# Chunked attention on one core: q and k transposed and split for pairs of heads, rows placed by DMA from the SyncE queue

## The chip, the cores and the metric

The kernel runs on one core of a Trainium2 chip. The metric is the device time of one execution in microseconds (us); the median of three runs of the kernel before is 1270.3 us (1268.56 to 1270.39). Engines are named as in the profile: PE is the matmul engine (PEld its weight loads), DVE is VectorE, ACT is ScalarE, POOL is GpSimd, SP is SyncE, which here only issues DMAs.

## The reference, cut to what matters

One layer of a transformer trunk on 1024 positions: a combined input projection, two groups of eight attention heads, an output projection, then a convolutional gated feed-forward layer. The two attention groups:

```python
# "mla": 8 heads, head dim 96, causal by 64-position chunks over all keys
s = einsum('bqhd,bkhd->bhqk', qb, k) * scale;  p = softmax(where(mask, s, NEG_INF));  o = p @ v
# "ca": 8 heads, head dim 64: each 64-position chunk sees itself and the 8 chunks before it
q, k = rmsnorm(q, g_ca_q), rmsnorm(k, g_ca_k)
s = einsum('bcqhd,bckhd->bhcqk', qc, kb) * scale
s = where(valid, s + rel_bias[:, clip(dist)], NEG_INF)
o = softmax(s) @ vb
...
x += concat(rmsnorm(o_a, g_out_mla), rmsnorm(o_b, g_out_ca)) @ w_out
x += conv_glu_ffn(rmsnorm(x))
```

## The kernel before, in words

Everything is float32. A product of two float32 tensors is made of three matmuls: each operand is split into a high part (rounded to the matmul's format) and a low part (the rest), and hi·hi, lo·hi and hi·lo are added in PSUM (`mm3`, lines 136 to 139). So every operand costs a rounding copy on ACT and a subtraction on DVE or POOL.

The program's order is written out by hand. The stages, with their time in the profile: latent projections and the mla up-projection (to 79 us), the projection to q, k and v of the chunked heads in 32 steps (79 to 230 us), attention (230 to 523 us), output projection (to 619 us), and the feed-forward layer, up (to 1051 us) and down (to the end).

**Attention** goes over 16 heads, `heads`, in turn ca and mla (n = 0 is ca head 0, n = 1 mla head 0, n = 2 ca head 1, ...). Each head has 12 score pieces; the program has one *slot* for each, 192 in all. In a slot PE makes the score piece (L908 to L922), ACT takes the exponential twice, a third engine forms the low part of the probabilities `plo` by a subtraction (L950: POOL from a copy in SBUF, or DVE from PSUM for the pieces listed in `PLO_V`), and PE adds the product of probabilities and v three slots later (L958 to L960, `LAG` is 3).

**Preparing a head** (`prep(n)`) is spread over the 24 slots ahead of its first score; slot m of head n's preparation is slot 12(n - 2) + m. For a ca head: 16 PE transposes of 128x64 blocks of q and k, in groups of four (L671); q's high part on ACT (L674) and low part on DVE (L678), k's likewise (L682, L688); 32 rows zeroed on POOL (`zero`, L694); q's high part copied to partitions 64 to 127 and k's high part to partitions 0 to 63 of a stacked tensor by two DMAs that POOL issues (`dup_q`, `dup_k`, L691 and L697). Then eleven passes `mx` multiply q with k (L737) and DVE takes row maxima from them (L745 for ca, L750 for mla). The maxima are transposed (L756), negated (L759) and put into a row of the operand set by a DMA that POOL issues (L760). Three operand sets `QH, QL, K1, K2` rotate over the heads; their mask rows are written once per set by ACT (`set_rows`, L612). The first two heads are prepared during the last steps of the chunked projection; their slots are given by `first_slot`, from -8 to 60.

**Ending a head** (`finish`): the sums of the exponentials are fetched by DMA (L1011), inverted on DVE (L1014), written to DRAM (L1016) and read back spread over 64 partitions (L1017); ten slots later DVE multiplies (L1023). Every second head of a kind, ACT squares the pair's outputs and DVE adds the squares up (`o_sq`, L978 and L979).

Each engine runs its instructions in order, and so does each DMA-issuing queue: a DMA on SP or POOL that waits for data holds back what stands behind it there.

## Time and profile before

| | |
|---|---|
| median of 3 runs | 1270.3 us (1268.56 to 1270.39) |
| profiled execution, its own time | 1271.62 us |
| its span from first to last instruction | 1269.9 us |
| busy PE / DVE / POOL / ACT | 1221.0 / 940.8 / 704.6 / 648.8 us |
| granted PE clock, mean over the span | 0.995 |

The span is what the trace covers; 1.7 us of the execution's time lie around it. A busy engine is one that executes an instruction; PE's matmuls are pipelined, so a busy PE can still differ in pace, and the granted clock (1 is 2.4 GHz, 0.5 is 1.2 GHz) has to be read beside it.

### The profile page before, as it was taken

What the parts mean: (1) busy time and instruction counts of PE and PEld (TensorE: products, weight loads), DVE (VectorE), ACT (ScalarE), POOL (GpSimd) and SP (SyncE); (2) the same over time, 40 slices, a digit from 0 to 9 for tenths busy, and PEclk for the clock granted to TensorE, in tenths of its full rate; (3) what the DMA queues carried; (4) which work ended last, traced back from release to release, by engine and by line L of the source; (5) the groups of instructions that cost most, each with busy time, mean ns of one, the idle gap of its engine ahead of it and who ended that gap; (6) DMA issues with size and microseconds to landing.
All of it is one profiled execution on the core that took longest, in us unless ns stands there. A gap on an engine that the chain in (4) does not pass through costs nothing.

```text
span 1269.9 us, 17774 instructions
## 1 busy us (share of the span) xinstructions
PE 1221.0 (96%) x5888; PEld 1004.7 (79%) x5888; DVE 940.8 (74%) x1623; ACT 648.8 (51%) x1338; POOL 704.6 (55%) x710
## 2 busy tenths in 40 slices
PE   9999998899998998999889999999999999999998
PEld 9888876787786876788668888888888888878887
DVE  6678565688888895466898766767776677888983
ACT  7562254678877887405555434334334344434442
POOL 4689750466564668204488767667677640425630
PEclk9999998999999999999999999999999999999999
DMA  9111213111111221265413332333322256933153
GB/s 353 36 35 50 59 56 78 26 44 43 27 37 37 43 64 52 100 232 174 141 59 121 120 99 84 108 108 105 119 81 86 91 181 243 363 92 116 59 197 127
DMA packets 102637, 134.78 MB, mean 106 GB/s; under 512 B 12152, under 2 KB 60816, under 8 KB 102544
## 3 DMA queue, kind: packets, MB, share of 16 engines
q1 hardware_dynamic: 100752, 129.37, 31.3%
q0 software_dynamic: 1792, 4.26, 1.7%
q8 instruction: 47, 0.77, 0.3%
q14 instruction: 46, 0.38, 0.1%
HBM read 97.47 MB, written 31.81 MB: 102 GB/s over the span
## 4 chain that ended last, share of the span: by engine, by line
PE 50%; DVE 8%; issue 2%; ACT 1%; POOL 1%; DVEq 0%; POOLq 0%; ACTq 0%
PE pb L139 11%; PE pb L138 11%; PE pb L137 11%; PE ps L137 6%; PE ps L139 5%; PE ps L138 5%; DVE ps L1438 1%; DVE as L1422 1%; DVE hq L1242 1%; POOL plo L950 1%; DVE wop L1359 1%; DVE h L1206 0%; DVE as L1421 0%; DVE as L1423 0%; DVE as L1424 0%
## 5 line engine op out<-in xcount | busy, mean ns | idle before, releaser
L950 POOL TENSOR_TENSOR plo<-misc,phi 128x512 fp32r<-128x512 f32 (+3 forms) x116 | 119.1, 1029 | 58.0 <-ACT phi L935 42.7
L1383 ACT ACTIVATE u<-ps,cols 128x1024 f32<-128x1024 f32 x44 | 53.2, 1208 | 178.0 <-DVE ps L1438 178.0
L137 PE MATMUL ps<-hq,wop 128*128 128x512 f32 x344 | 135.0, 393 | 2.6 <-ACT wop L1354 1.5
L139 PE MATMUL ps<-hq,wop 128*128 128x512 f32 x344 | 134.2, 390 | 1.8 <-DVE wop L1359 1.8
L138 PE MATMUL ps<-hq,wop 128*128 128x512 f32 x344 | 134.0, 390 | 0.2 <-DVE hq L1242 0.2
L138 PE MATMUL pb<-wring,aring 128*128 128x512 f32 x308 | 120.7, 392 | 2.1 <-DVE wring L1613 2.1
L137 PE MATMUL pb<-wring,aring 128*128 128x512 f32 x308 | 120.6, 391 | 0.3 <-DVE x2b L1438 0.3
L139 PE MATMUL pb<-wring,aring 128*128 128x512 f32 x308 | 120.6, 391 | 0.0
L1359 POOL TENSOR_TENSOR wop<-S,wop 128x512 fp32r<-128x512 f32 x42 | 63.3, 1507 | 96.4 <-ACT wop L1354 96.4
L137 PE MATMUL pb<-hq,wop 128*128 128x512 f32 x264 | 103.0, 390 | 2.3 <-ACT wop L1354 2.2
L139 PE MATMUL pb<-hq,wop 128*128 128x512 f32 x264 | 103.1, 390 | 0.2 <-DVE wop L1359 0.2
L138 PE MATMUL pb<-hq,wop 128*128 128x512 f32 x264 | 102.7, 389 | 0.0
L1610 DVE TENSOR_TENSOR aring<-ast,aring 128x512 fp32r<-128x512 f32 x77 | 71.1, 924 | 37.6 <-ACT aring L1609 37.6
L1609 ACT ACTIVATE aring<-ast 128x512 fp32r<-128x512 f32 x77 | 48.5, 630 | 93.7 <-PE pb L138 74.0
L932 ACT ACTIVATE misc<-pb 128x512 f32<-128x512 f32 (+3 forms) x116 | 56.3, 485 | 47.9 <-PE pb L918 20.0
L137 PEld LDWEIGHTS ps<-hq,wop 128*128 128x128 f32 x344 | 64.5, 188 | 20.0 <-DVE ps L1438 4.9
L138 PE MATMUL pb<-wl,hTh 128*128 128x512 f32 x192 | 75.8, 395 | 2.0 <-DVE wl L553 1.9
L139 PEld LDWEIGHTS ps<-hq,wop 128*128 128x128 f32 x344 | 64.6, 188 | 16.0 <-DVE wop L1359 2.5
L137 PE MATMUL pb<-wh,hTh 128*128 128x512 f32 x192 | 76.2, 397 | 0.0
L139 PE MATMUL pb<-wh,hTl 128*128 128x512 f32 x192 | 75.6, 394 | 0.0
L138 PEld LDWEIGHTS ps<-hq,wop 128*128 128x128 f32 x344 | 64.6, 188 | 13.7 <-DVE hq L1242 0.6
L204 POOL TENSOR_TENSOR stat<-stat,mhalf 128x1 f32<-128x1 f32 (+2 forms) x50 | 72.7, 1454 | 4.2
(331 smaller groups left out, 3629.8 us busy)
## 6 DMA issues: line engine op xcount, KB each, us to landing
wstage<-in_w_up_dram SPq DMA_DIRECT2D x43, 512.0 KB, 4.2
ast<-act_scratch SPq DMA_DIRECT2D x77, 256.0 KB, 4.5
act_scratch<-as SPq DMA_DIRECT2D x44, 256.0 KB, 2.3
wd<-in_w_down_dram SPq DMA_DIRECT2D x44, 256.0 KB, 5.5
act_scratch<-u SPq DMA_DIRECT2D x33, 256.0 KB, 2.1
x<-in_x_dram SPq DMA_DIRECT2D x16, 512.0 KB, 7.2
ws<-in_w_in_dram SPq DMA_DIRECT2D x32, 256.0 KB, 2.6
x_scratch<-x SPq DMA_DIRECT2D x14, 512.0 KB, 3.0
```

The source lines that it names most:

```text
L137: T.matmul(o, lh, rh, start=start, stop=False)
L138: T.matmul(o, lh, rl, start=False, stop=False)
L139: T.matmul(o, ll, rh, start=False, stop=stop)
L204: G.tensor_tensor(dst, dst, mhalf[:, :n], op=ALU.pow)
L932: A.activation(p32[:, w], o[:, w], AF.Exp, scale=sc_)
L950: e.tensor_tensor(plo[:, w], p32[:, w], f(phi[:, w]), op=ALU.subtract)
L1242: lo_eng.tensor_tensor(lo, s3[:, ks], f(hi), op=ALU.subtract)
L1359: (V if n in W_LO_V or (j, n) in W0_LO_V else G).tensor_tensor(lo, s, f(hi), op=ALU.subtract)
L1383: A.activation(u, U, AF.Identity, scale=convw(2, c), bias=convb(c))
L1422: V.tensor_tensor(s[1], s[0], A11, op=ALU.subtract)
L1609: A.activation(ah, s, AF.Copy)
L1610: V.tensor_tensor(al, s, f(ah), op=ALU.subtract)
```

## The change

Of the eight ca heads, h = 2 to 7 are prepared in pairs. The even head of a pair transposes 128x128 blocks, which hold both heads, and splits both heads' q and k at once into four staging tensors `qh, ql, kh, kl` with q and k of the even head on partitions 0 to 63 and of the odd head on 64 to 127. Each of the two heads then fetches its 64 partitions from the staging tensors by six DMAs. The odd head makes no transposes and no splits. Heads h = 0 and 1 are prepared as before. Beside that:

- DMAs that POOL issued in the attention (copies of q and k, the row of maxima) are issued by SP; the 32 zero rows come by DMA from a DRAM scratch instead of a POOL memset.
- Mask rows: POOL writes those of set 0, early; the other two sets get them from set 0 by DMA. ACT has none.
- The first head's `mx` passes use only the 64 rows of the high parts, and so read neither copy.
- The maxima passes of paired heads begin at slot 10 (even) or 7 (odd) of their preparation, not 9.
- For mla heads one more `plo` piece of 512 columns (piece 6) goes to POOL instead of DVE.
- `o_sq`: the addition comes three slots after the square (but for the last pair). `finish`: the read-back of the inverted sums is issued two slots later than the write.
- The loads of the projection's weights for steps 23 to 31 are issued one step earlier.

```diff
-PLO_V = (1, 3, 6, 8, 10)
+PLO_V = (1, 3, 6, 8, 10), (1, 3, 8, 10)
+WC_AHEAD = 20
+MX_EVEN = 10
+MX_ODD = 7
...
-    def set_rows(i):
-        st = sets[i]
+    def zero_rows():
+        st = sets[0]
+        G.memset(f(st.K2[64:96]), 0.0)
+        G.memset(f(st.QL[64:96]), 0.0)
+        nc.sync.dma_start(dzero, f(st.QL[64:96]))
+    def set_rows():
+        st = sets[0]
         for dst, c in ((st.K2, 0), (st.QL, 16)):
-            A.activation(dst[96:113].rearrange("p (t i) -> p t i", t=16),
-                         mk[96:113, c:c + 16, None].to_broadcast([17, 16, 64]), AF.Copy)
+            G.tensor_copy(dst[96:113].rearrange("p (t i) -> p t i", t=16),
+                          mk[96:113, c:c + 16, None].to_broadcast([17, 16, 64]))
+    def copy_rows(i):
+        r = 64 if heads[i][0] == "ca" else 96
+        nc.sync.dma_start(f(sets[i].K2[r:113]), f(sets[0].K2[r:113]))
+        nc.sync.dma_start(f(sets[i].QL[97:113]), f(sets[0].QL[97:113]))
...
+        def pair_tr(which, i):
+            p = hold[which, i] = bank()
+            for t in range(4):
+                T.transpose(p[:, t * 128:(t + 1) * 128], ca[which, h // 2][:, (4 * i + t) * 128:(4 * i + t + 1) * 128],
+                            ident)
+        def pair_hi(which, i):
...
+            A.activation(stg["kh" if which else "qh"][:, i * 512:i * 512 + 512], hold[which, i], AF.Copy,
+                         scale=1.0 if which else gsc[:, 1:2])
+        def pair_lo(which, i):
...
+        def send(x_):
+            o = f(stg[x_][64 * (h % 2):64 * (h % 2) + 64])
+            for d_ in {"qh": (st.QH[0:64], st.QH[64:128]), "ql": (st.QL[0:64],), "kh": (st.K2[0:64], st.K1[0:64]),
+                       "kl": (st.K1[64:128],)}[x_]:
+                nc.sync.dma_start(f(d_), o)
         def dup_q():
-            G.dma_start(st.QH[64:128], st.QH[0:64])
+            nc.sync.dma_start(f(st.QH[64:128]), f(st.QH[0:64]))
         def zero():
-            G.memset(f(st.QL[64:96]), 0.0)
+            nc.sync.dma_start(f(st.QL[64:96]), dzero)
...
-                q_, k2 = (st.QH, st.K1) if is_ca else (st.QH[0:d], st.K2[0:d])
+                q_, k2 = (st.QH, st.K1) if is_ca and n else (st.QH[0:d], st.K2[0:d])
...
-            G.dma_start(st.QL[96:97].rearrange("p (t s) -> p t s", t=8), mrow)
+            nc.sync.dma_start(f(st.QL[96:97]).rearrange("p (t s) -> p t s", t=8), f(mrow))
...
+        paired = is_ca and h > 1
+        if paired and h % 2:
+            mx_at = MX_ODD
+            r = [(0, "post", lambda: send("qh")), (1, "post", lambda: send("kh")), (2, "post", lambda: send("kl")),
+                 (3, "post", lambda: send("ql"))]
...
+            if paired:
+                mx_at = MX_EVEN
+                r += [(4, "post", lambda: send("qh")), (5, "post", lambda: send("kh")),
+                      (6, "post", lambda: send("kl")), (7, "post", lambda: send("ql"))]
...
-            micro[16, 9, 0, 0] = [lambda: set_rows(0)]
-            micro[26, 9, 0, 0] = [lambda: set_rows(1)]
+            micro[9, 9, 0, 0] = [set_rows]
+            micro[20, 9, 0, 0] = [lambda: copy_rows(1)]
...
-        return s % 12 in PLO_V if n < 14 else s in END_PLO_V
+        return s % 12 in PLO_V[n % 2] if n < 14 else s in END_PLO_V
...
+        if j < 3:
+            at(s0 + 3, add)
...
+        at(s + (5 if n < 14 else 3), spread)
```

The rows below are the program's own order, without times. The first two pieces are PE's around the first maxima pass of head 0, in step 26 of the chunked projection (`wh`, `wl` are its weights, `hTh`, `hTl` the input's parts, `set` an operand set); what an instruction waits for stands in brackets, DMASW being DMAs issued by POOL. Before:

```order
L138 MATMUL pb_2018<-wl_2046,hTh_96 128x512
L139 MATMUL pb_2018<-wh_2045,hTl_97 128x512
L737 MATMUL pb_2080<-set_2021 128x256 [waits DMASW1_49,DMASW0_49,DVE_49]
L737 MATMUL pb_2080<-set_2021 128x256
L737 MATMUL pb_2083<-set_2021 128x384
L137 MATMUL pb_2019<-wh_2045,hTh_96 128x512
```

and after, where the pass is on L783:

```order
L140 MATMUL pb_2020<-wl_2049,hTh_96 128x512
L141 MATMUL pb_2020<-wh_2048,hTl_97 128x512
L783 MATMUL pb_2085<-set_2023 128x256 x2
L783 MATMUL pb_2088<-set_2023 128x384
L139 MATMUL pb_2021<-wh_2048,hTh_96 128x512
```

The pass stands at the same place among the projection's matmuls; its wait for two DMAs is gone.

The next two pieces are POOL's while head 2 is scored and head 4 (the first even head of a pair) is prepared; `plo` is the low part of the probabilities, `vset` v's low part. Before:

```order
L950 TENSOR_TENSOR plo_2790<-misc_2284,phi_2766 128x512
L694 MEMSET set_2023 32x1024
L950 TENSOR_TENSOR plo_2838<-misc_2284,phi_2810 128x256
...
L709 TENSOR_TENSOR vset_2361<-nqk_604,vset_2361 128x128
L691 DMA set_2023<-set_2023 64x1024
L950 TENSOR_TENSOR plo_2895<-misc_2284,phi_2867 128x512
L697 DMA set_2023<-set_2023 64x1024
L950 TENSOR_TENSOR plo_2913<-misc_2284,phi_2892 128x512
L760 DMA set_2021<-mrow 1x8x128
L950 TENSOR_TENSOR plo_2946<-misc_2284,phi_2927 128x256
```

and after (L950 has become L1018, L709 L755):

```order
L1018 TENSOR_TENSOR plo_2790<-misc_2285,phi_2766 128x512
L1018 TENSOR_TENSOR plo_2840<-misc_2285,phi_2810 128x256
...
L755 TENSOR_TENSOR vset_2362<-nqk_604,vset_2362 128x128
L1018 TENSOR_TENSOR plo_2900<-misc_2285,phi_2869 128x512
L1018 TENSOR_TENSOR plo_2918<-misc_2285,phi_2897 128x512
L1018 TENSOR_TENSOR plo_2954<-misc_2285,phi_2933 128x256
```

The memset and the three DMAs that stood between the subtractions have left POOL.

The last two pieces are SP's at the same place: the bias table of head 4, the sums of head 1 (`den`) and their way through DRAM, and after the change the rows of head 4 out of the staging tensors. Before:

```order
L712 DMA misc_2284<-bias_scratch 128x256
L1011 DMA den<-misc_2284 128x1x8
L1016 DMA den_scratch<-den 128x8
L1017 DMA misc_2284<-den_scratch 64x1024
L712 DMA misc_2284<-bias_scratch 128x256
```

and after (L758 is the bias table, L740 the zero rows, L734 `send`, L806 the row of maxima of head 3, L1087 to L1094 the sums):

```order
L758 DMA misc_2285<-bias_scratch 128x256
L740 DMA set_2024<-zero_scratch 32x1024
L1087 DMA den<-misc_2285 128x1x8
L734 DMA set_2024<-stage_2822 64x1024 x2
L734 DMA set_2024<-stage_2881 64x1024 x2
L1091 DMA den_scratch<-den 128x8
L734 DMA set_2024<-stage_2882 64x1024
L758 DMA misc_2285<-bias_scratch 128x256
L806 DMA set_2023<-mrow 1x8x128
L734 DMA set_2024<-stage_2823 64x1024
L1094 DMA misc_2285<-den_scratch 64x1024
```

Five DMAs have become thirteen, and the read-back of the sums now stands behind the sends and the row of maxima.

## Rows read from the trace of the kernel before

**Rows 1.** Windows: length, busy PE, PEld, DVE, ACT, POOL; clock, DMA share, GB/s.

```profile
199.30:230.10 30.80, 24.12 (x105) 18.94 (x105) 17.18 (x51) 11.22 (x19) 0.65 (x2) 0.89 0.18 44
230.10:483.70 253.60, 237.79 (x1448) 192.69 (x1447) 213.25 (x575) 202.00 (x496) 155.97 (x203) 1.00 0.19 43
266.40:300.80 34.40, 33.33 (x211) 27.79 (x210) 28.82 (x81) 26.97 (x67) 21.10 (x30) 1.00 0.18 40
371.30:409.80 38.50, 34.66 (x211) 27.43 (x209) 33.72 (x87) 29.83 (x73) 20.72 (x29) 1.00 0.17 35
444.50:483.70 39.20, 35.07 (x210) 27.34 (x209) 34.61 (x85) 31.90 (x77) 28.92 (x37) 1.00 0.26 72
```

**Rows 2.** Timeline: PE's two waits for copies; start, us, what, idle before.

```profile
202.97 0.55 PE L737 MATMUL pb<-set 128*128 128x256 f32 x1 [3.61 <-DMA set<-set]
...
245.87 0.65 PE L737 MATMUL pb<-set 128*128 128x256 f32 x3 [1.05 <-DMA set<-set]
```

**Rows 3.** Busy time of 2 us stretches after the first wait; clock third from last.

```profile
202.00:204.00 2.00, 1.03 (x4) 1.07 (x5) 0.23 (x2) 0.61 (x1) 0.00 (x0) 0.50 0.46 136
...
208.00:210.00 2.00, 2.00 (x11) 1.64 (x11) 0.63 (x2) 0.75 (x2) 0.00 (x0) 0.80 0.29 106
```

**Rows 4.** Timeline, 212 to 216 us: ACT, DVE, PE.

```profile
212.07 2.00 ACT L612 ACTIVATE set<-mk 17x1024 fp32r<-17x1024 f32 x2
...
214.59 0.42 DVE L720 TENSOR_TENSOR bl<-tb,bh 128x256 fp32r<-128x256 f32 x1 [2.61 <-issue]
...
215.61 0.44 PE L737 MATMUL pb<-set 128*128 128x384 f32 x1 [1.63 <-DVE mcol L745]
```

**Rows 5.** Timeline of PE: one group of four transposes.

```profile
447.07 0.60 PE L671 MATMUL pb<-identr,ca 128*64 128x128 f32 x4
447.42 0.36 PE L908 MATMUL pb<-set 128*128 128x256 f32 x1
447.63 0.28 PE L916 MATMUL pb<-bh,identr 128*128 128x256 f32 x1
447.74 0.29 PE L916 MATMUL pb<-bl,identr 128*128 128x256 f32 x1
```

**Rows 6.** Timeline of PE: four transposes of 128x128 blocks, elsewhere.

```profile
610.30 0.63 PE L1256 MATMUL pb<-identr,h 128*128 128x128 f32 x4 [0.37 <-DVE h L1206]
```

**Rows 7.** Timeline of POOL and PE around two of PE's waits.

```profile
277.19 0.56 POOL L697 DMA_DIRECT2D set<-set  x1 [1.05 <-ACT phi L927]
...
279.10 0.45 PE L960 MATMUL pb<-plo,vset 128*66 128x512 f32 x1 [1.07 <-POOL plo L950]
...
422.75 0.45 PE L960 MATMUL pb<-plo,vset 128*66 128x512 f32 x1 [1.07 <-POOL plo L950]
```

**Rows 8.** Groups by form, 230 to 490 us: count, busy us, mean ns, idle before.

```profile
L950 POOL TENSOR_TENSOR plo<-misc,phi 128x512 fp32r<-128x512 f32 x50 | 66.6, 1333 | 43.0 <-ACT phi L935 30.3 <-PE pb L922 10.3 <-PE pb L960 2.2
...
L678 DVE SCALAR_TENSOR_TENSOR set<-pb,gsc,set 64x512 fp32r<-64x512 f32 x14 | 10.3, 733 | 0.0
...
L950 DVE TENSOR_TENSOR plo<-pb,phi 128x512 fp32r<-128x512 f32 x14 | 9.5, 680 | 0.9 <-ACT pb L928 0.9
...
L979 DVE TENSOR_TENSOR sqs<-sqs,sq 128x512 f32<-128x512 f32 x6 | 7.3, 1223 | 3.6 <-ACT sq L978 3.6
```

**Rows 9.** DMA issues: count, KB each, median us from issue to landing.

```profile
set<-set POOLq DMA_DIRECT2D x16, 256.0 KB, 3.0
...
misc<-den_scratch SPq DMA_DIRECT2D x16, 256.0 KB, 3.5
```

**Rows 10.** Timeline: last low part of head 4's k; its tenth slot.

```profile
276.92 0.68 DVE L688 TENSOR_TENSOR set<-pb,set 64x512 fp32r<-64x512 f32 x1 [0.74 <-ACT set L682]
...
280.80 0.28 PE L908 MATMUL pb<-set 128*128 128x256 f32 x1
```

**Rows 11.** Timeline: head 0's read-back issued, its first multiplication.

```profile
259.56 0.48 SPq L1017 DMA_DIRECT2D misc<-den_scratch  x1
...
267.21 0.69 DVE L1023 TENSOR_TENSOR op<-misc 64x512 f32<-64x512 f32 x1
```

More of the change, by code (lines that the diff above doesn't have):

```diff
@@ L650, in pieces @@
         return r
+    stg = {}
     def prep(n):
@@ L767, in prep @@
         if is_ca:
-            r += [(1, "post", zero), (4, "post", dup_q), (5, "post", dup_k), (-1, "post", lambda: bias_load(0)), (6, "post", bias_nat),
+            if n:
+                r += [(1, "post", zero)]
+            r += [(-1, "post", lambda: bias_load(0)), (6, "post", bias_nat),
                   (6, "post", lambda: bias_load(1)), (14, "post", bias_tr)]
         for j in range(11):
-            m = min((MX_CA if is_ca else 6) + max(j - 1, 0), 17)
+            m = min(mx_at + max(j - 1, 0), 17)
@@ L818, in trunk @@
     for i, (c, k, ts) in enumerate(steps):
-        if i + 2 < len(steps):
+        if i == WC_AHEAD:
             load_wc(i + 2)
+        if i + 2 + (i >= WC_AHEAD) < len(steps):
+            load_wc(i + 2 + (i >= WC_AHEAD))
         if i < 4:
@@ L891, in trunk @@
     new_set(2)
-    set_rows(2)
+    copy_rows(2)
     opair, O, wo, sqs = {}, {}, {}, {}
@@ L973, in o_sq, with add @@
             A.activation(sqs[kind][:, w], o, AF.Square)
-        else:
-            if c == 0:
-                opair["sq"] = blk(F32, "sq")
-            sq = opair["sq"][:, w]
-            A.activation(sq, o, AF.Square)
-            (G if (kind, j) in OSQ_G else V).tensor_tensor(sqs[kind][:, w], sqs[kind][:, w], sq, op=ALU.add)
+            return
+        if c == 0:
+            opair["sq"] = blk(F32, "sq")
+        sq = opair["sq"][:, w]
+        A.activation(sq, o, AF.Square)
+        def add():
+            (G if (kind, j) in OSQ_G else V).tensor_tensor(sqs[kind][:, w], sqs[kind][:, w], sq, op=ALU.add)
+        if j < 3:
+            at(s0 + 3, add)
+        else:
+            add()
     def o_part(kind, j, c):
@@ L1014, in rec, with spread @@
             V.reciprocal(d8, d8)
-            row = dden[n]
-            nc.sync.dma_start(row.rearrange("(p c) -> p c", c=8), d8)
-            nc.sync.dma_start(R[64:128], dap(row, 0, [[0, 64], [1, 1024]]))
+            nc.sync.dma_start(dden[n].rearrange("(p c) -> p c", c=8), d8)
+        def spread():
+            nc.sync.dma_start(R[64:128], dap(dden[n], 0, [[0, 64], [1, 1024]]))
         def mul(c):
```

54 lines of the change are left out of this document (36 added, 18 removed).

## The prediction

> **What bounds the kernel now.** I read the windows first, because the change touches one part of the program, the end of the chunked projection and the attention. In the attention's main stretch PE is busy 237.8 of 253.6 us, DVE 213.3, ACT 202.0 and POOL 156.0 [rows 1]. So PE sets the pace there, with 15.8 us of idle time, and DVE at 84% is the next engine. Time comes off the end in two ways: PE work that goes away, and PE waits that go away. Two pairs of heads look different from the rest: heads 2 and 3 leave PE idle 34.40 - 33.33 = 1.1 us, heads 8 and 9 3.8 us and heads 12 and 13 4.1 us [rows 1]. The stretch before, 199.3 to 230.1, in which the last projection steps and the preparation of heads 0 and 1 lie, is worse: 24.1 of 30.8 us busy at a mean clock of 0.89, while no other engine is busy more than 17.2 us [rows 1]. It is a chain of waits, not a full engine.
>
> Then the timeline, for what ends these waits. The first maxima pass of head 0 waits 3.61 us for a copy that POOL issued, and a pass of head 2 waits 1.05 us for another [rows 2]. After the first of them the clock stands at 0.50 from 202 us and at 0.80 in 208 to 210 [rows 3]: some 6.8 us at 1.2 GHz, in which PE does 3.4 us less than at 2.4. At 215.61 PE waits 1.63 us for DVE, which had stood still 2.61 us until ACT wrote a bias tile, and ACT had spent 2.0 us just before on the mask rows of L612 [rows 4]. In the attention POOL, in order, stands 1.05 us before the DMA of L697, the subtraction behind it comes late, and PE waits 1.07 us at 279.10 [rows 7]. There are four such waits of 0.9 to 1.07 us, in heads 2, 4, 6 and 10, the last at 422.75.
>
> **Term 1, the first stretch: 7.5 us.** The first pass no longer waits for the copies, so the 3.61 us go, and with them the clock's 3.4. ACT no longer writes mask rows (POOL does; it is busy 0.65 us in this stretch, so that costs nothing), so the wait at 215.61 should go: 1.6. That is 8.6. I take 7.5, as something else may become late: the weights of the next step came in at about the same time as the copy. They are now ordered a step earlier, which is why I don't take less. Bounds: 3, if those weights stop PE instead; 10.1, if PE works without a wait (30.8 minus the 24.1 less 3.4).
>
> **Term 2, transposes: 5.4 us.** Three pairs of heads make 16 transposes each where they made 32: 48 fewer, 12 groups of four. From the first transpose of a group at 447.07 to the matmul after next at 447.63 are 0.56 us, of which the matmul between takes 0.11 (447.63 to 447.74) [rows 5]: 0.45 a group, 12 of them 5.4. As busy time the same group counts 0.60, so 7.2 is the upper bound; the lower, if PE's time here is not what holds the end, is a rival below. The transposes that stay are twice as wide in their weights. Four of 128x128 take 0.63 us elsewhere, against 0.60 for four of 128x64 [rows 5, 6], so I add nothing.
>
> The Trainium skill speaks against that: "TensorE: Matmul & The Clock Gate", in the section on LDWEIGHTS, gives the load a time of columns / 1.2 in ns, so 107 instead of 53 ns for the wide blocks. Were the loads what paces them, the 48 transposes left would cost 2.6 us more and term 2 would be 2.8. The trace does not agree: 0.63 against 0.60 us for four.
>
> **Term 3, DMAs off POOL: 5 us.** The four waits of rows 7 and head 2's wait of 1.05 us [rows 2] come from POOL's order, and no DMA and no memset is left between its subtractions. In exchange POOL makes seven subtractions of 512 columns more, 1.33 us each [rows 8], one in each mla head; it has 97 us idle in the stretch [rows 1] and the new piece lies between pieces that were already its own, so I price them at nothing. If the cover is too thin, each could cost PE what a late one costs now, 1.07. Bounds 0 to 5.2.
>
> **Term 4, less work on DVE and later sums: 3.5 us.** Twelve splits of 0.73 us on 64 partitions go (24 become 12 of 128 partitions; the time goes by columns), 8.8 us, and seven subtractions of 0.68, 4.8 us [rows 8]. That is 13 of DVE's 213 us, worth nothing in itself, as DVE is not the bound. But heads 8, 9, 12 and 13 are those in which the sums of squares run: six additions of 1.22 us, before which DVE stands 3.6 us for ACT's squares [rows 8]. These four heads have 8.0 - 2 x 1.1 = 5.8 us more idle PE time than heads 2 and 3. The additions now come three slots (4.3 us at 34.4 / 24 a slot) after the squares, so DVE doesn't stand; they still cost their 1.22 us each. I take 3.5 of a possible 0 to 5.8.
>
> **Term 5, new waits: -2 us.** The low part of k is the last thing that an even head sends. In head 4 it was ready at 277.60, and slot 10, after which the first pass now comes, began at 280.80 [rows 10]. The pass itself starts some 0.5 us later, at 281.3, but 1.1 us earlier once the wait at 279.10 is gone: 280.2. A DMA takes 3.0 us to land [rows 9] and the queue some 0.5: 281.1. So 0.9 us late in each of three even heads, less what DVE gains by term 4: I take 2 in all, bounds 0 to 6. An odd head sends everything in slots 0 to 3 and begins in slot 7, four slots or 5.7 us later, which covers it. The mask rows of sets 1 and 2 are sent well ahead of their heads' scores; the zero rows also lie in slot 1 of 24. Nothing for these.
>
> Sum: 7.5 + 5.4 + 5 + 3.5 - 2 = 19.4. From the profiled execution's own 1271.6 that leaves 1252.2. The median of the runs is 1.3 us below the profiled one; I leave that inside the range and say **1252 us**. What follows the attention is PE work that only starts earlier.
>
> **The rivals.**
> - *The attention is held by DVE and ACT, not by PE.* For it: 84% and 80% [rows 1], and each slot's chain passes through both. Against it: in heads 2 and 3 PE idles 1.1 us of 34.4. Then terms 2 and 4 give nothing: 7.5 + 5 - 2 = 10.5, **1261 us**.
> - *The first stretch only changes what it waits for,* so that the change there doesn't do what it says: the weights of the next step land at the time at which the copy did. Term 1 is then 1 and the time **1259 us**.
> - *Everything in the two stretches goes that can go:* 10.1 + 7.2 + 5.2 + 5.8 = 28.3, **1243 us**.
> - *SP's queue becomes the late one.* The read-back of a head's sums was issued at 259.56, lands 3.5 us later, and is used at 267.21: 4.1 us of cover [rows 9, 11]. Two slots later (2.9 us) leave 1.2, and it now stands behind the sends and the row of maxima. If these hold it 2 us, DVE stands 0.8 us in each of 14 heads; if all of it reaches PE, 11 us are lost: **1263 us**.
> - *Slower.* In the slots 4 to 7 of an even head six copies of 256 KB go out together. If the last needs not 3.0 but 6.0 us to land, the pass in slot 10 is 3.9 us late, the clock falls as after the first wait in rows 2 and 3 (3.4 us), and three times 7.3 take 22 of the 21.4 us that the other terms give: no change. From there it decides; at 7 us it is 25, and **1275 us**. Against it: the DMA share in the attention is 0.19 [rows 1].
>
> **How the numbers follow.** Forecast 0.60; DVE and ACT hold 0.13; first stretch 0.07; everything goes 0.10; SP's queue 0.05; slower or level 0.05. The range runs from the best case to a little beyond the queue's: **1243 to 1264**, which leaves out the last rival and part of the queue's and of the best case's spread. A measurement here can tell 0.2%, 2.5 us, from no change. All cases but the last are faster by more than that; of it and the tails of the others I give 0.05 to no change and 0.03 to slower: 0.92, 0.05, 0.03.
>
> **What the profile after would show.** Term 1: no wait of PE over 1 us around 200 us, no half clock there, the first score 7 to 9 us earlier. Term 2: 80 transposes of q and k of ca heads instead of 128, and PE's busy time in the attention 5 us lower. Term 3: no wait of PE for POOL in heads 2, 4, 6 and 10. Term 4: heads 8, 9, 12 and 13 with 2 us of idle PE time or less a pair. Term 5: PE waits for the sent rows at the first pass of heads 4, 8 and 12, of about 1 us. Wrong I would be if a wait of several us stands at one of those three passes, if PE waits for weights near 203 us, or if DVE waits for the read-back in each head.

## The result and the profile after

Eight timed executions of the changed kernel have a median of 1261.2 us (1257.1 to 1266.5), eight of the kernel before on the same chip 1272.3 us (1268.6 to 1274.0). The ratio is 0.9914, interval 0.9899 to 0.993: about 11 us faster. 1252 us were forecast, with a range of 1243 to 1264. The profiled execution of the changed kernel took 1257.13 us (span 1255.4), its fastest.

Windows of the changed kernel (length, busy PE, PEld, DVE, ACT, POOL, clock, DMA share, GB/s): the 30.8 us ahead of the first score, the attention from there to head 14, heads 2 and 3, 6 and 7, 8 and 9, 12 and 13.

```profile
193.20:223.96 30.76, 29.47 (x128) 20.76 (x127) 22.17 (x59) 10.92 (x22) 2.69 (x4) 1.00 0.23 65
223.96:468.48 244.52, 231.11 (x1401) 190.14 (x1399) 197.04 (x551) 193.12 (x482) 141.88 (x173) 0.99 0.32 75
257.01:294.45 37.44, 34.84 (x210) 29.07 (x209) 28.72 (x79) 26.75 (x67) 18.93 (x25) 0.95 0.31 68
327.15:363.55 36.40, 33.31 (x211) 27.98 (x209) 28.38 (x79) 26.77 (x67) 18.96 (x25) 1.00 0.31 71
363.55:395.80 32.25, 31.93 (x195) 26.17 (x193) 27.45 (x79) 27.72 (x69) 19.40 (x25) 1.00 0.34 77
431.69:468.48 36.79, 33.41 (x195) 25.84 (x193) 28.79 (x77) 29.97 (x73) 26.53 (x29) 1.00 0.43 111
```

Against [rows 1] the first score comes at 223.96 in place of 230.10 with the clock at 1.00 in place of 0.89; the attention is 9.1 us shorter; heads 8 and 9 take 32.25 us where they took 38.50, with 0.3 us of idle PE where there were 3.8. But heads 2 and 3 take 37.44 where they took 34.40. There, and in heads 6 and 7 and 10 and 11, which also prepare the even head of a pair, time was lost.

The timeline of PE in the changed kernel, at the first maxima pass of heads 4, 8 and 12 (start, us, instruction, idle time before it and what ended it):

```profile
273.41 0.65 PE L783 MATMUL pb<-set 128*128 128x256 f32 x3 [2.60 <-DMA set<-stage]
...
344.04 0.65 PE L783 MATMUL pb<-set 128*128 128x256 f32 x3 [3.09 <-DMA set<-stage]
...
412.15 0.68 PE L783 MATMUL pb<-set 128*128 128x256 f32 x3 [2.50 <-DMA set<-stage]
```

`set<-stage` is a transfer of `send`: PE waits 8.2 us in all for rows of an even paired head. What is late shows in the same stretch in SP's queue (the x4 are q's high part twice and k's high part twice, the x1 at 269.48 is k's low part, L806 the row of maxima of head 3), on DVE, and in the DMA share (second to last column):

```profile
264.22 4.50 SPq L734 DMA_DIRECT2D set<-stage  x4
268.82 0.56 SPq L1091 DMA_DIRECT2D den_scratch<-den  x1
269.48 1.27 SPq L734 DMA_DIRECT2D set<-stage  x1
270.84 0.54 SPq L758 DMA_DIRECT2D misc<-bias_scratch  x1
271.47 0.70 SPq L806 DMA_DIRECT2D set<-mrow  x1
```

```profile
267.62 0.69 DVE L724 TENSOR_TENSOR stage<-pb,stage 128x512 fp32r<-128x512 f32 x1 [0.81 <-ACT stage L717]
...
269.25 0.27 DVE L805 TENSOR_SCALAR mrow<-pb 8x128 fp32r<-8x128 f32 x1
```

```profile
266.00:268.00 2.00, 2.00 (x16) 1.00 0.95 195
...
270.00:272.00 2.00, 0.80 (x7) 1.00 1.00 199
272.00:274.00 2.00, 0.59 (x4) 1.00 0.93 196
274.00:276.00 2.00, 2.00 (x10) 0.53 0.77 199
276.00:278.00 2.00, 2.00 (x8) 0.61 0.05 10
```

k's low part is ready at 268.31 (267.62 + 0.69), is issued 1.2 us later and has landed at 273.4, 5.1 us after it was ready. All DMA engines are busy in that time, at 195 to 199 GB/s: at that rate a transfer of 256 KB takes 1.3 us, and k's low part is the third in a row of them. After the wait the clock stands at 0.53 and 0.61.

### The profile page after: what moved, and what is told of

The parts are those of the page before. It is cut to its first block, busy times and chain, and to the rows that moved or that the text cites. A ratio compares the mean times of both kernels' runs of the same rounds, so it can differ in the third digit from the quotient of the medians.

```text
span 1255.4 us, 17692 instructions
## 1 busy us (share of the span) xinstructions
PE 1215.1 (97%) x5840; PEld 1001.0 (80%) x5840; DVE 927.3 (74%) x1603; ACT 636.1 (51%) x1320; POOL 691.2 (55%) x680
## 3 DMA queue, kind: packets, MB, share of 16 engines
q1 hardware_dynamic: 104730, 141.37, 35.9%
## 4 chain that ended last, share of the span: by engine, by line
PE 50%; DVE 7%; POOL 2%; issue 2%; ACT 1%; DMA 0%; SPq 0%; POOLq 0%; DVEq 0%; ACTq 0%
PE pb L140 11%; PE pb L139 11%; PE pb L141 11%; PE ps L139 6%; PE ps L141 5%; PE ps L140 5%; DVE as L1500 1%; DVE ps L1516 1%; DVE as L1499 0%; DMA ast<-act_scratch 0%; POOL hq L1320 0%; DVE wring L1691 0%; DVE as L1501 0%; DVE as L1502 0%; DVE h L1284 0%
## 5 line engine op out<-in xcount | busy, mean ns | idle before, releaser
L1018 POOL TENSOR_TENSOR plo<-misc,phi 128x512 fp32r<-128x512 f32 (+3 forms) x123 | 126.7, 1033 | 77.7 <-ACT phi L1003 52.2
L141 PE MATMUL ps<-hq,wop 128*128 128x512 f32 x344 | 134.2, 390 | 1.2 <-DVE wop L1437 1.2
L140 PE MATMUL ps<-hq,wop 128*128 128x512 f32 x344 | 134.0, 390 | 0.1
L140 PE MATMUL pb<-wring,aring 128*128 128x512 f32 x308 | 120.9, 393 | 2.3 <-DVE wring L1691 2.3
L141 PE MATMUL pb<-wring,aring 128*128 128x512 f32 x308 | 120.3, 391 | 0.0
L141 PE MATMUL pb<-hq,wop 128*128 128x512 f32 x264 | 103.6, 392 | 0.1
L140 PE MATMUL pb<-hq,wop 128*128 128x512 f32 x264 | 103.3, 391 | 0.0
L1000 ACT ACTIVATE misc<-pb 128x512 f32<-128x512 f32 (+3 forms) x123 | 60.6, 493 | 52.7 <-PE pb L986 24.0
L140 PE MATMUL pb<-wl,hTh 128*128 128x512 f32 x192 | 75.1, 391 | 2.0 <-DVE wl L555 2.0
L141 PEld LDWEIGHTS ps<-hq,wop 128*128 128x128 f32 x344 | 64.6, 188 | 15.2 <-DVE wop L1437 1.8
L140 PEld LDWEIGHTS ps<-hq,wop 128*128 128x128 f32 x344 | 64.6, 188 | 13.8 <-DVE hq L1320 0.6
L141 PE MATMUL pb<-wh,hTl 128*128 128x512 f32 x192 | 74.9, 390 | 0.0
```

The source lines that it names most:

```text
L140: T.matmul(o, lh, rl, start=False, stop=False)
L141: T.matmul(o, ll, rh, start=False, stop=stop)
L1000: A.activation(p32[:, w], o[:, w], AF.Exp, scale=sc_)
L1018: e.tensor_tensor(plo[:, w], p32[:, w], f(phi[:, w]), op=ALU.subtract)
```

## The experiments

Theory A: the part of the gain that is missing is this lateness, because transfers of 256 KB follow one another at 1.3 us each; and the clock that falls behind the waits in some executions makes the spread. Rivals: the wait only moves on, or something else than the transfers comes last.

All ratios are to the kernel before on the same chip. Eleven kernels that differ from the changed one and one more set of executions of it were run.

**e1_even12.** The passes of even heads begin two slots later.

```diff
-MX_EVEN = 10
+MX_EVEN = 12
```

> Edit: the changed kernel with the maxima passes of even chunked heads two units later (slot 12 in place of 10); nothing else. Theory A (the part of the gain that is missing is PE waiting for the low part of k, which is sent too late: 2.60 + 3.09 + 2.50 = 8.2 us at the first passes of heads 4, 8 and 12 in the profile of the changed kernel, and the clock that falls behind them in some executions): those three waits go or shrink below 0.5 us each, the time is 1249 to 1253 us, a ratio to before of 0.982 to 0.985, and the executions lie closer together than 1257 to 1266. Rival B (the wait only moves on: with two units less, VectorE reaches the maxima too late and PE waits for the row of maxima at the end of the same heads, or at the next head's first scores): the waits come back there, 2 to 3 us in each of the three heads, and the time stays at 1257 to 1266 us. Rival C (the spread and the missing part come from elsewhere): the waits go but the time falls by under 3 us.

1266.3 us (1263.6 to 1269.7), ratio 0.9959 (0.9945 to 0.9973): slower than the changed kernel, so theory A as I had it missed, and B is right on what happens. The waits at the passes are gone, but PE waits 2.0, 2.9 and 2.1 us at the first piece of the next head, for its row of maxima. In this kernel's timeline of PE, and of SP ahead of the first of them:

```profile
277.17 0.50 PE L990 MATMUL pb<-set 105*128 105x512 f32 x1 [2.02 <-DMA set<-mrow]
```

```profile
272.36 1.25 SPq L734 DMA_DIRECT2D set<-stage  x1
273.70 0.54 SPq L758 DMA_DIRECT2D misc<-bias_scratch  x1
274.33 0.70 SPq L806 DMA_DIRECT2D set<-mrow  x1
```

That row was ready at 272.40 and was issued at 274.33, behind k's low part. So in the changed kernel two things are late for the same reason, one behind the other, and the first wait hides the second. Behind two of the three waits the clock falls to 0.50 to 0.65. That alone does not make this kernel slower than the changed one, whose clock falls too: heads 2 and 3 take 37.69 us here with the clock at 1.00 throughout, against 37.44 there at 0.95, and PE has further waits of 0.72 and 0.31 us for DVE's maxima at 281.76 and 284.37. No run takes these apart from the rest.

**e2_order.** One transfer less ahead of k's low part.

```diff
-"ql": (st.QL[0:64],), "kh": (st.K2[0:64], st.K1[0:64]),
+"ql": ((st.QL[0:64], "ql"), (st.K2[0:64], "kh")), "kh": ((st.K1[0:64], "kh"),)
```

> Edit: the changed kernel with SP's queue in another order only: at even chunked heads the copy of the high part of k into the second tile goes out last, with the low part of q, so that one issue less stands ahead of the low part of k. Theory A (the low part of k is late, and part of that is SP's queue: in the profile of the changed kernel it was ready at 268.31 and issued at 269.48 while two copies and a scratch write were issued ahead of it): it is issued 0.5 to 1 us earlier, the three waits of 2.5 to 3.1 us become 1.5 to 2.5 us, and the time falls by 2 to 4 us against the changed kernel, to 1256 to 1260 us in the median. Rival D (what is late is the transfer, not its place in the queue): the waits stay at 2.5 us or more, same time as the changed kernel (1259 to 1263 us).

1259.5 us (1256.7 to 1264.0), ratio 0.991 (0.9894 to 0.9927). The waits are 1.23, 1.90 and 1.16 us: less by 1.2 to 1.4 each, which is one transfer at 1.3. That speaks for A (the wait follows what stands ahead in the queue) and against D; the median fell by 1.7 us only, within what these runs can tell from nothing.

**e3_nopair.** No pairs.

```diff
-        paired = is_ca and h > 1
+        paired = False
```

> Edit: the changed kernel without the pairing: every chunked head transposes and splits its own rows again (48 transposes more), with copies inside the head and maxima passes at the place of the unpaired heads. First stretch, SP's queue for the copies and the later sums of squares stay as changed. Theory A: the transposes (5.4 us by the prediction's sum) and VectorE's splits come back, the three waits of 8.2 us for the low part of k go, so the pairing as it stands is worth about nothing or less than 3 us: 1258 to 1264 us. Rival E (VectorE's or ScalarE's load is what the pairing takes off the path, as well as the transposes): 1266 to 1270 us, with PE waiting for VectorE at the rows of maxima of the heads from 2 on.

1258.4 us (1258.1 to 1260.3), ratio 0.9904 (0.9891 to 0.9916): A. Taking the pairing out leaves the time where it was and the executions within 2.2 us. Two of its windows, heads 4 and 5, and heads 8 and 9:

```profile
291.24:326.18 34.94, 34.06 (x211) 27.86 (x209) 29.90 (x81) 29.55 (x73) 19.43 (x25) 1.00 0.18 44
360.64:395.53 34.89, 34.16 (x210) 27.79 (x209) 30.37 (x82) 29.56 (x73) 19.82 (x25) 1.00 0.17 42
```

The changed kernel takes 32.7 and 32.25 us there, in which the odd heads of pairs are prepared without transposes: 2.2 and 2.6 us gained, PE's busy time lower by 2.2 each. What the pairing gives there it loses in heads 2, 3, 6, 7, 10 and 11, in which the even heads of pairs are prepared and wait for their rows. The kernel without pairs has six waits of its own at first passes, 0.4 to 1.0 us and 4.0 in all; the trace puts five of them down to copies from SP and one to ACT.

**e4_rows128.** Head 0's passes on all 128 rows, as before the change.

```diff
-q_, k2 = (st.QH, st.K1) if is_ca and n else (st.QH[0:d], st.K2[0:d])
+q_, k2 = (st.QH, st.K1) if is_ca else (st.QH[0:d], st.K2[0:d])
```

> Edit: the changed kernel with all maxima passes of head 0 on 128 rows (both copies) in place of 64. Theory A1 (the 64-row passes of head 0 cost PE about 0.1 us at each change between 64 and 128 rows, 2.7 us over 12 passes, and this is why the first stretch gave 6.1 us and not 7.5): the spacing of matmuls around each visit falls from 0.33 to 0.23 us, but the first pass waits for the copies by DMA, as in the kernel before, where the two waits were 3.61 and 1.05 us: together +1 to +3 us against the changed kernel, 1261 to 1265 us, and the first score stands at 224 to 227 us. Rival F (the number of rows costs nothing, the spacing has another reason): spacing stays, only the wait comes, 1264 to 1267 us.

1259.4 us (1255.3 to 1262.7), ratio 0.9908 (0.989 to 0.9926): no difference that can be told, where I had expected a loss. The first pass waits 0.85 us only. The trace names DVE's low part of the weights for that wait, but this was ready at 201.37 and the pass began at 202.26, so it was likely a copy, which SP now issues. And the spacing of the matmuls is as A1 says. PE's timeline around a visit to a pass, in the changed kernel and in this one:

```profile
199.80 0.40 PE L141 MATMUL pb<-wh,hTl 128*128 128x512 f32 x1
200.13 0.49 PE L783 MATMUL pb<-set 64*128 64x512 f32 x1
200.55 0.50 PE L139 MATMUL pb<-wh,hTh 128*128 128x512 f32 x1
200.89 0.40 PE L140 MATMUL pb<-wl,hTh 128*128 128x512 f32 x1
```

```profile
203.21 0.40 PE L141 MATMUL pb<-wh,hTl 128*128 128x512 f32 x1
203.44 0.39 PE L783 MATMUL pb<-set 128*128 128x512 f32 x1
203.68 0.39 PE L139 MATMUL pb<-wh,hTh 128*128 128x512 f32 x1
203.90 0.39 PE L140 MATMUL pb<-wl,hTh 128*128 128x512 f32 x1
```

From L141 to L140 behind the pass, 1.09 us with 64 rows, 0.69 with 128. From the first pass to the first score it is 25.3 us (198.63 to 223.96) against 23.1 (202.26 to 225.32): 2.3 us, less the 0.85 of the wait.

**a_again.** The changed kernel once more, beside the next three.

> Edit: none, the changed kernel itself, beside the next three on one chip. It is to give the ratio that it had (0.9914, 0.9899 to 0.993) and the same spread of its executions (1257 to 1266 us). If it lies above the kernel without pairing (0.9904 on the chip of the first experiments) by 1 to 3 us and spreads more, the pairing as it was made costs what the three waits and the clock behind them cost.

1261.4 us (1256.3 to 1264.9), ratio 0.992 (0.9899 to 0.9941). This time the profile is of an execution of 1264.9 us, and it shows where the spread is from. Its clock (third column from the end) at 50 us, in the latent projections, which the change does not touch, and behind the first two of the three waits (behind the third it is 0.50 too, at 420 us):

```profile
48.00:50.00 2.00, 0.00 (x0) 1.00 0.00 0
50.00:52.00 2.00, 1.58 (x6) 0.51 0.00 0
...
276.00:278.00 2.00, 2.00 (x8) 0.50 0.94 239
...
350.00:352.00 2.00, 2.00 (x6) 0.50 0.09 25
```

In the first profile the clock stood at 1.00 at 50 to 52 us, and below 1 only behind the first of the three waits. The first of these passes starts at 275.97 in place of 273.41, 2.6 us later; head 14's first score at 476.55 in place of 468.48, 8.1 us later. So 5.5 us of the difference between two executions of one kernel lie behind waits of nearly the same length. The other 2.5 us lie ahead of the first score: near 50 us PE's stall is 2.80 us long here and 1.18 in the first profile, and the clock falls behind the longer one only.

**e6_kfirst.** Pairs do k before q; the transfers that passes don't read go last.

```diff
+                tr_ = lambda w, i: pair_tr(1 - w, i)
...
-                r += [(4, "post", lambda: send("qh")), (5, "post", lambda: send("kh")),
-                      (6, "post", lambda: send("kl")), (7, "post", lambda: send("ql"))]
+                r += [(4, "post", lambda: send("kh")), (5, "post", lambda: send("kl")),
+                      (5, "post", lambda: send("qh")), (6, "post", lambda: send("kh2")),
+                      (7, "post", lambda: send("ql"))]
```

> Edit: the changed kernel with pairs that transpose and split k first and q after it, so that the low part of k is sent a slot earlier; the copy of k's high part into the second tile and the low part of q, which the maxima passes don't read, go out last; head 0's passes on 128 rows. The passes stay at slot 10, so the row of maxima is not later than in the changed kernel. Theory A (what the pairing loses is only the lateness of the sent rows, 5 us after they are ready, behind four other transfers of 256 KB): the waits at the first passes of heads 4, 8 and 12 go from 2.5 to 3.1 us to below 0.5, no wait for the row of maxima comes in their place, and the time is 1247 to 1251 us, a ratio of 0.980 to 0.984, with all executions within 3 us. Rival B (the wait moves on wherever the passes stand, because the transfers of an even head take the queues for most of the slots between): a wait of 1.5 us or more for the rows of q at the same passes, or for the row of maxima, and 1255 to 1260 us.

1260.7 us (1255.7 to 1263.6), ratio 0.9909 (0.9886 to 0.9931): a miss. The passes now wait 1.33, 1.30 and 1.25 us for the last of four transfers, q's second copy, and the row of maxima is held on SP as before. In this kernel's timeline:

```profile
275.49 0.36 PE L783 MATMUL pb<-set 128*128 128x256 f32 x1 [1.33 <-DMA set<-stage]
...
279.01 0.50 PE L991 MATMUL pb<-set 105*128 105x512 f32 x1 [1.18 <-DMA set<-mrow]
```

k's low part is one transfer, q's high part is two: what was won by sending k early was spent on the second one. Heads 6 and 7 took 36.4 us together, as in the changed kernel, so B is right on what happens here, though each wait is a little under its 1.5 us.

**e7_pooldma** and **e8_oldsq** take one more term out of the kernel without pairs.

```diff
-            nc.sync.dma_start(f(st.QH[64:128]), f(st.QH[0:64]))
+            G.dma_start(st.QH[64:128], st.QH[0:64])
...
-            nc.sync.dma_start(f(st.QL[64:96]), dzero)
+            G.memset(f(st.QL[64:96]), 0.0)
```

> Edit: the kernel without pairing (1258.4 us), with the copies of q and k and the row of maxima issued by POOL again and the 32 zero rows a POOL memset again. The prediction's term 3: POOL's order holds its subtractions back again, with PE waits of 0.9 to 1.1 us in each ca head from 2 on, together 4 to 6 us slower than the kernel without pairing: 1262 to 1265 us (ratio 0.993 to 0.996). Rival G (those waits were spare, something else ends at the same time): less than 2 us slower.

```diff
-PLO_V = (1, 3, 6, 8, 10), (1, 3, 8, 10)
+PLO_V = (1, 3, 6, 8, 10), (1, 3, 6, 8, 10)
...
-        if j < 3:
+        if j < 0:
             at(s0 + 3, add)
```

> Edit: the kernel without pairing (1258.4 us), with the additions of the squares right behind the squares and five subtractions in every mla head on VectorE, as in the kernel before. The prediction's term 4, without its part from the splits: waits of PE for VectorE come back in heads 8, 9, 12 and 13, together 2 to 4 us: 1260 to 1262.5 us (ratio 0.992 to 0.994). Rival H (VectorE has cover enough, the two edits are worth nothing): within 1 us of the kernel without pairing. If term 3 and term 4 together give less than the 13 us that the kernel without pairing gains, less some 6 us of the first stretch, the remaining difference belongs to the mask rows and the first stretch.

e7_pooldma took 1263.9 us (1260.8 to 1265.2), ratio 0.9938 (0.9921 to 0.9955), e8_oldsq 1262.7 us (1260.7 to 1264.8), ratio 0.9932 (0.9916 to 0.9949). Against the kernel without pairs (0.9904) the DMAs on POOL cost 4.3 us by the ratios, 5.5 by the medians, the other two edits 3.6 and 4.3. Both show the waits that the prediction named. PE's timeline of the first and of the second:

```profile
270.36 0.45 PE L1028 MATMUL pb<-plo,vset 128*66 128x512 f32 x1 [1.08 <-POOL plo L1018]
```

```profile
372.99 0.27 PE L802 MATMUL pb<-identr,mcol 128*8 128x128 f32 x1 [1.74 <-DVE mcol L799]
```

There are six waits on POOL of 0.92 to 1.08 us in heads 2, 4, 6, 8, 10 and 12 in the one; in the other PE waits 1.7 us in heads 8 and 12 for the maxima that it transposes, where the changed kernel has 0.45 at most.

**e9_early, e10_mx11 and e12_slot** are made from what e1, e2 and e6 showed. The first sends in the order of e2, everything one slot earlier, and both transfers that no pass reads behind the row of maxima; e10 has this order and the later passes in place of the earlier slot; e12 the earlier slot alone. All three have head 0's passes on 128 rows.

```diff
+                r = [(m - 1, p, fn) for m, p, fn in r]
-                r += [(4, "post", lambda: send("qh")), (5, "post", lambda: send("kh")),
-                      (6, "post", lambda: send("kl")), (7, "post", lambda: send("ql"))]
+                r += [(3, "post", lambda: send("qh")), (4, "post", lambda: send("kh")),
+                      (5, "post", lambda: send("kl")), (9, "post", lambda: send("kh2")),
+                      (10, "post", lambda: send("ql"))]
```

> Edit: the changed kernel with transposes, splits and sends of even chunked heads one slot earlier, the two transfers that the maxima passes don't read (k's high part into the second tile, low part of q) moved to slots 9 and 10, and head 0's passes on 128 rows; the passes stay at slot 10. Theory A in its sharper form (each transfer of 256 KB takes all DMA engines for about 1.3 us, at some 195 GB/s; the low part of k waits behind those issued ahead of it, and the row of maxima of the mla head waits on SP behind it: in the changed kernel that row was ready at 269.5 and issued at 271.47, so taking only one of the two waits away lays the other bare): one transfer less ahead (1.3 us) and one slot (1.4 us) take 2.5 to 3.1 us down to below 0.5, the row of maxima is issued within 0.7 us of being ready, heads 2 and 3 take 34.0 to 34.6 us together in place of 36.4 to 38.7, no clock falls there, and the time is 1250 to 1254 us (ratio 0.983 to 0.987). Rival B (the pair of an even and the next head takes 36.4 us whatever is moved, since VectorE's bunched work or another row comes last): heads 6 and 7 together stay at 36 us or more and the time at 1257 to 1261 us.

> Edit: as the run before, but transposes, splits and sends stay in their slots and the passes come one slot later (11). The copy of k's high part into the second tile and the low part of q go out in slots 10 and 11. Theory A: the waits at the sent rows shrink to 0 to 0.5 us, the row of maxima of the next mla head is issued at once and costs less than 0.5 us, 1250 to 1255 us. What the later passes may cost: VectorE's maxima bunch against the row of maxima of the chunked head, 0.5 us a head, so that this run is 1 to 2 us behind the one with earlier sends. Rival B: as there, 1257 to 1261 us.

> Edit: the changed kernel with transposes, splits and sends of even chunked heads one slot earlier and head 0's passes on 128 rows, but all six transfers in the order of the changed kernel (the second copy of k's high part ahead of the low part of k, the low part of q in the slot behind it). With the run of the other order (1.3 us less at each wait) and the one with both (waits gone) this makes a square of two edits. Theory A (transfers one after another at 1.3 us each): waits at the first passes of heads 4, 8 and 12 are 1.0 to 1.8 us, the slot alone being worth 1.4 us; the clock falls behind some of them; 1254 to 1259 us, between the changed kernel and the run with both edits. If the slot alone were enough (waits below 0.5 us): 1250 to 1253 us, and the order would be worth nothing.

e9_early: **1251.4 us** (1250.5 to 1255.6), ratio 0.9842 (0.9822 to 0.9861). e10_mx11: 1255.9 us (1253.1 to 1256.2), 0.9867 (0.9852 to 0.9882). e12_slot: 1256.9 us (1254.6 to 1259.4), 0.9882 (0.9863 to 0.99). Order and slot make a square, though not a clean one, as e9 also holds two transfers back to later slots; the three waits at the passes together are 8.2 us with neither, 4.3 with the order, 3.3 with the slot, and with both there is no gap over 0.15 us left there. The slot alone also leaves 0.4 to 0.7 us at each next row of maxima. Windows of e9_early, from the first score to head 14's, heads 2 and 3, heads 6 and 7; and its SP queue, in which the row of maxima is ready at 271.87 and issued at 272.19:

```profile
225.97:465.30 239.33, 230.76 (x1400) 188.95 (x1399) 197.43 (x551) 193.23 (x482) 141.56 (x173) 1.00 0.33 77
...
259.60:294.02 34.42, 33.90 (x210) 27.86 (x209) 28.53 (x79) 26.82 (x67) 18.93 (x25) 1.00 0.33 74
326.72:361.05 34.33, 33.80 (x210) 27.90 (x209) 27.98 (x80) 26.82 (x67) 18.96 (x25) 1.00 0.35 76
```

```profile
265.57 4.62 SPq L734 DMA_DIRECT2D set<-stage  x4
270.28 0.53 SPq L1093 DMA_DIRECT2D den_scratch<-den  x1
271.09 1.01 SPq L758 DMA_DIRECT2D misc<-bias_scratch  x1
272.19 0.71 SPq L806 DMA_DIRECT2D set<-mrow  x1
273.62 0.48 SPq L1096 DMA_DIRECT2D misc<-den_scratch  x1
274.15 1.23 SPq L734 DMA_DIRECT2D set<-stage  x2
```

The same bytes are moved (142.5 MB in either), and PE no longer waits for them at these passes. Not all of it is gain. From the first score to head 14 e9_early is 5.2 us shorter than the changed kernel's first profile, though the three pairs of heads in which even heads are prepared are 7.6 shorter: heads 0 and 1 take 0.6 us more and heads 12 and 13 1.4 more. In these two groups PE waits 1.22 us for a copy at 239.10 and 1.03 us for a subtraction of DVE at 448.57. DVE waits 4.5 us for the read-back of the sums in heads 3, 7, 11 and 13 (1.7 in the changed kernel), which SP issues right ahead of the two sends that were held back, in head 13 ahead of a load of weights; the last of these waits is shortly before that second wait of PE:

```profile
443.86 0.92 DVE L1102 TENSOR_TENSOR op<-misc 64x512 f32<-64x512 f32 x1 [1.24 <-DMA misc<-den_scratch]
```

```profile
448.57 0.31 PE L685 MATMUL pb<-identr,nqk 128*96 128x128 f32 x1 [1.03 <-DVE plo L1020]
```

That the one brings about the other no run shows. e10 was dearer than expected: 1.08 us of wait stay at head 8, and 0.2 to 0.5 for rows of maxima.

**e11_first.** All undone but the first stretch: the prediction's term 1 alone.

```diff
-        paired = is_ca and h > 1
+        paired = False
...
-        at(s + (5 if n < 14 else 3), spread)
+        at(s + 3, spread)
```

with the edits of e7_pooldma and e8_oldsq.

> Edit: the changed kernel with everything but the first stretch undone: no pairing, copies, zero rows and row of maxima issued or made by POOL, additions of squares, subtractions and read-back as before. What stays: mask rows by POOL and DMA, head 0's passes on 64 rows, weights a step earlier. The prediction's term 1 alone. By the profile of the changed kernel its first score came 6.1 us earlier than before, of which 0.7 had come about ahead of 199 us: 1264.5 to 1267 us, a ratio of 0.994 to 0.997. By the prediction 7.5: 1263.8. Rival (the terms overlap, and what the other edits gave includes some of it): 1268 us or more.

1265.6 us (1263.2 to 1266.5), ratio 0.9945 (0.9927 to 0.9962): 6.2 us by the medians, 7.0 by the ratio.

## Why the prediction was right, and where it was not

The time lay inside the range and the sign was right; the forecast itself, 1252.2, was 9 us too low. Four of the five terms came out within 2 us of their size, as they were measured, and the fifth carries the miss. That the range held the time is in part luck: what took it up to 1264 were rivals at 1259, 1261 and 1263 us, and none of these is what happened, while the rival with the right mechanism was left outside it.

**Term 1, 7.5 us: 6.2 to 7.0, for the reason given.** The wait of 3.61 and the half clock of [rows 2, 3] are gone, and so is the wait at 215.61 [rows 4]; at 216.91 there are 0.53 us. The weights did not become late in this profile; in those of a_again, e4, e9 and e11 PE waits 0.7 to 0.8 us near 192 us for their low part, which DVE makes. I had not reckoned with the passes on 64 rows: they slow PE at each change from 128 rows to 64 and back, 2.3 us in all between e4 and the changed kernel. As e4 shows, the copies from SP come nearly in time anyway, so those 64 rows were worth little.

**Term 2, 5.4 us: about 6.2.** PE's busy time is 2.2 us lower than in the kernel without pairs in heads 4 and 5 and in heads 8 and 9, in which odd heads are prepared, and the time falls by 2.2 and 2.6 us with it. In heads 12 and 13 that kernel can't be used, as its clock stood at 0.50 for the last 2.8 us; e7_pooldma, which has no pairs either and a clock of 1.00 there, has 35.21 us of busy PE time against 33.40 in the changed kernel, 1.8 more. From the first score to head 14 e9_early has 6.9 us less busy PE time than the kernel without pairs (230.76 against 237.63), and its span there is 6.8 shorter (239.33 against 246.16); by an estimate 1.4 us of each are that half clock (half of 2.8). So the size lies between the forecast and its upper bound of 7.2. The rival that DVE and ACT hold the attention is refuted by this: PE is busy 34.06 of 34.94 us in heads 4 and 5 of the kernel without pairs, and what goes away of its work comes off the end. In the changed kernel a group of transposes reads:

```profile
L711 PE MATMUL pb<-identr,ca 128*128 128x128 f32 x48 | 7.2, 272 | 0.0
L685 PE MATMUL pb<-identr,ca 128*64 128x128 f32 x16 | 2.4, 272 | 0.0
```

These are groups by form, with the mean ns of one behind the busy time: 272 for the wide and the narrow block, and four of either take 0.60 us, as the prediction had it. Their weight loads, which run beside the matmuls, read:

```profile
L711 PEld LDWEIGHTS pb<-identr,ca 128*128 128x128 f32 x48 | 6.0, 140 | 0.9
L685 PEld LDWEIGHTS pb<-identr,ca 128*64 128x64 f32 x16 | 1.8, 111 | 0.4
```

The Trainium skill ("TensorE: Matmul & The Clock Gate", the section on LDWEIGHTS) lets the load go by columns, which would be an estimated 53 ns more for the wide block. The trace agrees that the load grows with the columns, but by 29 ns; it does not pace the transposes here.

**Term 3, 5 us: 4.3 to 5.5**, by e7_pooldma, with the waits of [rows 7] at their old length. **Term 4, 3.5 us: 3.6 to 4.3** by e8_oldsq, in which the part from the splits is not contained. Its statement on heads 12 and 13 was wrong: they keep 3.4 us of idle PE time. There POOL has taken DVE's place:

```profile
466.78 0.45 PE L1028 MATMUL pb<-plo,vset 128*66 128x512 f32 x1 [1.09 <-POOL plo L1018]
```

This is PE's timeline of the changed kernel in head 13, one of four such waits of 0.17 to 1.09 us. The seventh subtraction that POOL makes more was priced at nothing; e8_oldsq, without it, waits less for POOL there (0.41 us at most) but more for DVE. What e11, e7 and e8 show adds to 14 to 17 us, and the kernel without pairs has 12 to 13. These sizes hold for taking one term out of that kernel. Seen from e11_first the same edits give less: the edits of term 4 alone (e7 against e11) 0.9 to 1.8 us, those of term 3 alone (e8 against e11) 1.7 to 3.0, each with the later read-back, and both together 5.2 to 7.3, where the prediction has 8.5. Each ratio is known to some 2 us, so it is not shown that the terms depend on each other, nor how the two divide.

**Term 5, -2 us: this is the step that failed.** The place was right, k's low part at slot 10 of three even heads, and that it lands late; what failed is the landing of 3.0 us, and with it the size. (It is the last transfer that the passes read, not the last that is sent.) The profile has 8.2 us of waits in place of 2, and a wait of several us at these passes is what the prediction itself named as its sign of being wrong. What they cost with the clock behind them shows beside e9_early, which does the same work without them: the three pairs of heads in which even heads are prepared take 37.4, 36.4 and 35.9 us in the profiled execution against 34.4, 34.3 and 33.4, 7.6 us more; in the execution of a_again, with the clock at half behind each wait, 38.75, 39.20 and 37.43, 13.2 more. Where the clock does not fall a wait costs its length or less: in the first profile 2.5 us for 2.50 in heads 10 and 11, 2.1 for 3.09 in heads 6 and 7. Why the second is less, no run shows. The step took "A DMA takes 3.0 us to land" from [rows 9], a median over copies that went out one or two at a time, and set against the rival of a long landing the DMA share of 0.19 [rows 1], a mean over 250 us. In the slots in question the change itself brings 1.5 MB, the share is 0.93 to 1.00, and transfers go one after another at 1.3 us: 5.1 us from ready to landed, where the step put 3.5. The Trainium skill ("DMA: Bandwidth & Descriptors", Specifications) gives 435 GB/s as the ceiling of the fabric at SBUF; at that rate a transfer would take an estimated 0.6 us. These copies of 64 partitions from SBUF to SBUF stayed at 195 to 199 GB/s at a share near 1, less than half of the ceiling, and e2, in which one transfer less is worth 1.2 to 1.4 us, confirms the trace's 1.3. Other transfers of this kernel come near the ceiling: loads from DRAM into 128 partitions ran at 416 GB/s at a share of 1.03 from 22 to 24 us. Whether the 64 partitions or the source in SBUF makes the difference, no run here shows.

The rival that the first stretch only changes its wait is out by term 1. SP's queue was late, as another had it, but little for the read-back (DVE waits 1.7 us for it in all, in four heads): it was late for the row of maxima, which the prediction did not follow past the sends (ready at 269.5, issued at 271.47). And the slower rival was the true mechanism at a third to three fifths of its price: it put 6 us from issue to landing and 22 us in all, where the low part of k took 5.1 from ready to landed and the cost was 7.6 to 13.2.

So the sum comes out like this: e9_early has 20.6 us, of which some 1.4 are, by the trace of e4, head 0's passes on 128 rows (2.3 less the wait of 0.85); the other 19.2 are the change without late rows, against 21.4 in the prediction (7.5 + 5.4 + 5 + 3.5). Less 7.6 that is 11.6, less 13.2 it is 6.0: the changed kernel's executions lie 6 to 15 us below the median of before, 11 in the median. The sum closes to within some 3 us and no better: the execution that lost 7.6 lies 14.5 below the profiled one of before. The 2.0 us that e9_early loses itself, in heads 0, 1, 12 and 13, would be most of that difference.

## What to carry to other kernels

A copy that replaces engine work has to be priced at the DMA share of its own slots after the change, with its bytes in it, not at the mean share of the stage or the landing of a lone transfer: here 1.3 us for each 256 KB that stands ahead. Send what the next instruction reads first and put off what nobody reads yet, and follow the small transfers that stand behind on the same queue; a wait can hide a second one of the same length, so an edit that removes it (e1) may gain nothing until both causes are gone. The kernel to take is e9_early, the same change with the sends reordered: 0.9842 (0.9822 to 0.9861); what is left in it to look at first is DVE's wait for the read-back of the sums.

## What the runs showed of the hardware

- Of the 36 issues of `send` on SP in the changed kernel 30 take 0.46 to 0.74 us and six 1.24 to 1.63, each of the six behind three or four such transfers of 256 KB issued in the 5.3 us before it; what stands behind waits for that too. Not every issue in such a place is long: the write of the sums at 268.82 took 0.56.
- A matmul with 64 rows of weights between such with 128 spaces PE at 0.33 to 0.42 us where 512 columns otherwise take 0.23: 0.40 us for one visit. Matmuls with 113 rows between such with 128 show none of this in the same trace (0.11 to 0.13 us apart at 256 columns, from 260.15 on).
- The same stall of PE, 2.5 to 3.3 us, is followed by a clock of 0.50 for some microseconds in one execution and not in another: behind all three waits in one profile of the changed kernel, behind one in the other. In the kernel without pairs it stood at 0.50 behind a wait of only 1.07 us (467.13). Near 50 us, far from the change, the stall itself differs, 1.18 us in the first profile and 2.80 in a_again, and the clock with it, so part of the spread of these kernels lies outside the change.
